# Loading the prompt in eight pieces between the first wide tile's weights, and the gates' tile third

## The chip, the cores and the metric

One core of one Trainium2 chip runs the kernel. The metric is device microseconds of one execution of the whole program. A core has a matmul engine (TensorE, PE in the profile; its weight loads are PEld), VectorE (DVE), ScalarE (ACT), GpSimd (POOL) and SyncE (SP). SP and POOL issue nearly all DMAs here. Each engine takes its own instructions in the order in which the program wrote them and waits on semaphores for the others.

## What is computed

One inference step of a hybrid decoder layer, for a prompt of 512 tokens and a sample group of 32 tokens (8 sequences of 4), in float32, which share the weights:

```python
h = rmsnorm(x, norm_in)                                   # (544, 2048)
z = jnp.einsum('btd,dc->btc', h, w_in)                    # combined input projection
q_n, kv_n, g_n, z_n, q_f, k_f, v_f, f_f, z_f = jnp.split(z, cuts, axis=-1)
gates = jax.nn.sigmoid(g_n + b_gate)                      # 24 columns
logf = jax.nn.log_sigmoid(f_f + b_forget)                 # 8 columns
...                                                       # sparse attention (8 heads), forgetting attention (8 heads)
mix = jnp.concatenate([o_n * jax.nn.silu(z_n), o_f * jax.nn.silu(z_f)], axis=-1)
y = rmsnorm(x + jnp.einsum('btc,cd->btd', mix, w_out), norm_final)
```

The sample group also reads paged caches through a page table (indirect DMAs and DMAs of whole pages).

## The kernel before

**Numbers.** A float32 matmul is written as three matmuls in a faster format: both operands are split into a high part and a low rest (`h_hi`, `h_lo` for the tokens, `whi`, `wlo` for the weights), and `mm3` adds hi x hi, hi x lo and lo x hi.

**Tiles.** The input projection is a list of tiles of 128 output columns each (`tiles`, built by `add_in`). A tile has the 544 tokens in two halves of 272 (`hf`, `HALF`), the 2048 inputs in 16 k-steps (`kk` within `c`, four each), and so 2 x 16 x 3 = 96 wide matmuls into two PSUM banks (`pz`). Tile 0 is different: it holds the 24 gate columns and 8 forget columns, its weights `w_0` are loaded by POOL, and it is multiplied in plain float32, four k-steps side by side on 32 output rows each. Tiles 1 to 4 are keys and values of the sparse branch, tiles 5 to 8 the queries q0 to q3 of the forgetting branch.

**Weights.** The weights of a wide tile come in four slabs of 256 KB (`raw`, five buffers, number m = 4 t + c), loaded by `w_dma` on SP. `w_split(m, 0)` makes `whi` on ACT, `w_split(m, 1)` makes `wlo` on DVE and issues the load of the slab five further on. Slabs are split `W_AHEAD` = 2 ahead of their use.

**Start.** `start` loads the prompt (`xt`), turns it by TensorE transposes (four of 128x128 for each k-step, into a PSUM bank), and from each bank ACT writes `h_hi` and DVE `h_lo`, scaled with the norm's weights. The per-token factor of the RMS norm is left out of `h`; it is made beside it (`ss`, sums of squares; `rstd_of`, Newton steps; `dg` and two matmuls, which copy it over all rows: `rsb`) and multiplied into a tile's result `zt` as it leaves PSUM. A tile that ends before `rsb` is there is copied raw and multiplied later in `post` (`raw_part`).

**Order.** The program is one pass in Python that writes the instructions. `Clock` keeps an estimate of each engine's time, by formulas. `Streams` holds generators for everything beside the tiles; `pump()` continues those whose flags, tests and estimated ready times have come, by the estimated time of TensorE, and `need(...)` lets that time pass until flags are set. A `yield` with nothing waits for the estimated end of what the generator has just issued. So flags such as "x15" (k-step 15 has been written) or "t0" order what is *written*; on the chip only the order within an engine and the semaphores of real data dependences hold. `clock.parts` tells the estimate which parts of a buffer are tracked apart.

**Before, at the start:** `run_tiles(0, n_in)` takes the tiles in the order 0, 1, 2, ... Tile 0 begins when the first four k-steps are there ("begun"), and its c-th quarter needs k-steps 4c to 4c+3. `index_tiles` (page table arithmetic for the gathers) issues the loads of `w_0` first of all. The sums of squares are issued after tile 0 ("t0"), two on DVE, the others on ACT. Tile t is begun when tile t-2's `post` has set its flag, since `zt` has two buffers. `post_gf` turns tile 0's result into gates and forget values, on which `fox_sample_setup` waits ("gf").

Of the kernel before, what the change touches and what calls it, by code (L numbers as in the profile page):

```python
# [8 lines left out]
F32 = mybir.dt.float32  # L9
# [3 lines left out]
OP = mybir.AluOpType  # L13
# [27 lines left out]
class Clock:  # L41
# [19 lines left out]
    def keys(self, ap):  # L61
        k, part = self.key(ap), self.parts.get(ap.tensor.name)
        if not part:
            return [k]
        pitch, step = part
        lo = ap.offset % pitch
        hi = lo + sum(st * (n - 1) for st, n in list(ap.ap)[1:])
        return [(*k, i) for i in range(lo // step, hi // step + 1)]
# [232 lines left out]
def trunk_step(ctx, tc, x_prompt, x_sample, cache_nsa_kv, cache_fox_kv, cache_fox_logf, state_nsa_win,  # L301
# [127 lines left out]
    by_rows(h_hi), by_rows(h_lo)  # L429
# [83 lines left out]
    def run_tiles(t0, t1):  # L513
        for t in range(t0, t1):
            spec = tiles[t]
            if t == 0:
                S.need("begun")
            if t - 2 >= 0:
                S.need(f"post{t - 2}")
# [7 lines left out]
            for c in range(4):  # L527
                m = t * 4 + c
                if t == 0:
                    S.need(*[f"x{c * 4 + kk}" for kk in range(4)])  # L530
                    for hf, cut in enumerate(cuts):
                        sl = slice(*cut)
                        for b in (h_hi, h_lo):
                            for kk in range(4):
                                mm(ps[hf][kk * 32:kk * 32 + 32], w_0[0][:, m * 4 + kk], b[:, c * 4 + kk, sl].bitcast(F32),
                                   c == 0 and b is h_hi, c == 3 and b is h_lo)
                            S.pump()
                    w_split(m + W_AHEAD, 0)
                    w_split(m + W_AHEAD, 1)
                    if c == 3:  # L540
                        for hf, cut in enumerate(cuts):
                            cp(zt[:, slice(*cut)], ps[hf])
                        flags.add("t0")
                    S.pump()
                    continue
                hi, lo = wsp.pop(m)
                for hf, cut in enumerate(cuts):
                    sl = slice(*cut)
                    for kk in range(4):
# [3 lines left out]
                        if kk == 3 and c == 3:  # L553

                            if t > 1:
                                S.need("rsb")
                            elif t == 1:
                                raw_part.append(sl)
                            late = max(clock.t["dve"], clock.t["pe"]) > max(clock.t["act"], clock.t["pe"]) + 0.2
                            if t == 1:  # L560
# [12 lines left out]
            def post(t=t, spec=spec, zt=zt, raw_part=raw_part):  # L573
                yield [zt]
                if t == 1:
                    yield "rsb"
                for sl in raw_part:
                    nc.vector.tensor_tensor(zt[:, sl], zt[:, sl], rsb[:, sl], op=OP.mult)
                if raw_part:
                    yield [zt]  # L580
                yield from spec["post"](zt)
                flags.add(f"post{t}")
            S.add(post(), front=True)
            S.pump()

# [1300 lines left out]
    def start():  # L1886
        with tile_pool("pre") as pre:
            gn = load(pre.tile([KT, P], F32, name="gn"), dram(norm_in, 0, [[P, KT], [1, P]]))
            xs = load(pre.tile([32, D], F32, name="xs0"), dram(x_sample, 0, [[D, 32], [1, D]]))
            xt = pre.tile([P, 4, 4, 512], F32, name="xt")  # L1890
            clock.parts[xt.tensor.name] = (4 * D, D)
# [13 lines left out]
            jk = lambda n: pre.tile([P, 4, 512], F32, name="jk" + n)  # L1905
# [13 lines left out]
            for k in range(KT):  # L1919
                c = k // 4  # L1920
                if k % 4 == 0:
                    yield [xt[:, c]]
# [3 lines left out]
                for i in range(4):  # L1926
                    nc.tensor.transpose(tp[:, i * P:(i + 1) * P], xt[:, c, i, (k % 4) * P:(k % 4 + 1) * P], ident)
# [32 lines left out]
    def index_tiles():  # L1960
        ptb = big().bitcast(I32)[:, :64]
        pid = fsk.tile([64, 1], I32, name="pid")
        w_0.append(fx.tile([P, 1040], F32, name="ft", bufs=2)[:, :512].rearrange("p (k n) -> p k n", n=32))
        for (col, n, at) in tiles[0]["cols"]:
            nc.gpsimd.dma_start(w_0[0][:, :, at:at + n], dram(w_in[0], col, [[w_in.shape[-1], P], [P * w_in.shape[-1], KT], [1, n]]))
# [12 lines left out]
        yield "x11"  # L1978
# [11 lines left out]
        yield "t0"  # L1990
# [49 lines left out]
    if True:  # L2040
# [45 lines left out]
        run_tiles(0, n_in)  # L2086
# [30 lines left out]
```

## Time and profile before

| | |
|---|---|
| median of three runs | 1316.84 us (1313.9 to 1319.7) |
| the profiled execution | 1315.31 us |
| its span, first to last instruction | 1313.6 us |
| mean granted TensorE clock | 0.992 |
| TensorE busy | 1273.6 us, 97% of the span |
| VectorE, ScalarE, GpSimd busy | 60%, 42%, 21% |
| HBM | 235.68 MB read, 36.49 MB written |

Rows of the profile that stand below: a row of stretches gives the stretch, its length, the busy time of PE, PEld, DVE, ACT and POOL with the number of instructions, the granted TensorE clock, the share of the 16 DMA engines that was busy (it can pass 1 by a little) and the GB/s moved. A row of a timeline gives start and length in us, the engine (a q behind it is the engine's sequencer, which issues DMAs), the line, the operation, output<-inputs, shapes, the count, and in brackets how long the engine was idle before it and what ended that. A row of the chain of waits gives start, length and what held the chain then. All lines are L169, since one helper issues every instruction. A plain float32 matmul shows as two records.

### The profile page before, as it was taken

To read this page: it belongs to the slowest core of one execution; us is meant where nothing else is said; L and a number is where in the kernel's file an instruction comes from. 1 tells how busy PE (TensorE), PEld (TensorE's weight loads), DVE (VectorE), ACT (ScalarE), POOL (GpSimd) and SP (SyncE) were. 2 spreads that over 40 slices of the span, in tenths; PEclk is the share of its full clock that TensorE was granted. 3 is DMA by queue.
4 is the path that set the end of the run, shared out by engine and by line. 5 is a ranking of instruction groups with operands and counts; after the bars stand their busy time and mean duration, and the time that the engine had idled before them with its cause. 6 is when DMAs were issued, how large, how long until landed. Compare 5 with 4: busy or idle time off the path is not lost.

```text
span 1313.6 us, 27307 instructions
## 1 busy us (share of the span) xinstructions
PE 1273.6 (97%) x10149; PEld 1136.0 (86%) x10149; DVE 792.3 (60%) x1982; ACT 545.8 (42%) x1163; POOL 280.2 (21%) x357
## 2 busy tenths in 40 slices
PE   7999999999999999998999999899999999999997
PEld 5899998878989999998899988788888898777786
DVE  5836787775545667656687653666575255345256
ACT  4324333333334577741345551357654323333221
POOL 3312376644310000005661013011211000000000
PEclk8999999999999999999999999899999999999999
DMA  7576699989987455459987489996986693334423
GB/s 195 160 195 187 194 289 278 280 239 285 295 249 172 124 154 161 146 150 327 287 254 207 106 261 257 228 224 188 265 209 181 203 326 109 110 113 135 134 75 137
DMA packets 303665, 265.66 MB, mean 202 GB/s; under 512 B 83058, under 2 KB 250850, under 8 KB 302860
## 3 DMA queue, kind: packets, MB, share of 16 engines
q1 hardware_dynamic: 279372, 187.30, 51.1%
q0 software_dynamic: 24016, 76.10, 18.2%
q8 instruction: 79, 1.29, 0.4%
q14 instruction: 54, 0.44, 0.1%
q10 hardware_dynamic: 144, 0.52, 0.1%
HBM read 235.68 MB, written 36.49 MB: 207 GB/s over the span
## 4 chain that ended last, share of the span: by engine, by line
PE 73%; DMA 11%; issue 5%; DVE 4%; POOL 3%; SPq 2%; ACT 2%; POOLq 0%; DVEq 0%; ACTq 0%
PE pz L169 40%; PE po L169 15%; PE tr L169 5%; PE s L169 4%; PE accv L169 3%; PE acc L169 3%; DMA fpg<-in_cache_fox_kv 2%; DMA raw<-in_w_in 2%; POOL fpg L169 2%; DMA fpg<-in_cache_fox_kv,fi 2%; SPq L169 2%; PE accf L169 1%; PE psb L169 1%; DMA fvz<-out 1%; POOL crow L169 1%
## 5 line engine op out<-in xcount | busy, mean ns | idle before, releaser
L169 PE MATMUL pz<-h_hi,whi 128*128 128x272 f32 x1920 | 567.1, 295 | 7.0 <-ACT zt L169 6.4
L169 PE MATMUL pz<-h_hi,wlo 128*128 128x272 f32 x1920 | 555.3, 289 | 3.4 <-DVE wlo L169 3.4
L169 PE MATMUL pz<-h_lo,whi 128*128 128x272 f32 x1920 | 553.9, 289 | 0.0
L169 PEld LDWEIGHTS pz<-h_hi,whi 128*128 128x128 f32 x1920 | 362.7, 189 | 24.6 <-issue 14.4
L169 PEld LDWEIGHTS pz<-h_hi,wlo 128*128 128x128 f32 x1920 | 362.1, 189 | 4.3 <-DVE wlo L169 4.3
L169 PEld LDWEIGHTS pz<-h_lo,whi 128*128 128x128 f32 x1920 | 363.3, 189 | 0.8
L169 ACT ACTIVATE whi<-raw 128x512 fp32r<-128x512 f32 x275 | 171.4, 625 | 236.3 <-PE pz L169 118.7
L169 DVE TENSOR_TENSOR wlo<-raw,whi 128x512 fp32r<-128x512 f32 x275 | 185.9, 677 | 136.9 <-ACT whi L169 134.5
L169 POOL DMA_INDIRECT fpg<-in_cache_fox_kv,fi x128 | 129.7, 1014 | 294.8 <-DMA out<-nat 208.2
L169 DVE STREAM_TRANSPOSE ft<-fpg 128x1024 f32<-128x1024 f32 x64 | 78.5, 1231 | 42.0 <-DMA fpg<-in_cache_fox_kv,fi 36.7
L169 PE MATMUL po<-whi,h_hi 128*128 128x512 f32 (+1 forms) x256 | 95.6, 374 | 0.0
L169 DVE TENSOR_TENSOR zt<-pz,rsb 128x272 f32<-128x272 f32 x67 | 29.6, 441 | 107.9 <-PE pz L169 105.9
L169 PE MATMUL po<-wlo,h_hi 128*128 128x512 f32 (+1 forms) x256 | 94.0, 367 | 0.0
L169 PE MATMUL po<-whi,h_lo 128*128 128x512 f32 (+1 forms) x256 | 93.9, 367 | 0.0
L169 POOL DMA_INDIRECT crow<-in_cache_nsa_kv,ci x64 | 66.3, 1036 | 114.3 <-DVE ct L169 89.8
L169 ACT ACTIVATE cxh<-ct 128x580 fp32r<-128x580 f32 (+1 forms) x64 | 42.2, 660 | 107.2 <-DVE ct L169 92.8
L169 POOL DMA_DIRECT2D spg<-in_cache_nsa_kv x64 | 35.0, 546 | 183.8 <-DVE skt L169 74.0
L169 PEld LDWEIGHTS po<-whi,h_hi 128*128 128x128 f32 x256 | 48.1, 188 | 20.1 <-ACT whi L169 7.6
L169 POOL DMA_DIRECT2D fpg<-in_cache_fox_kv x64 | 35.0, 552 | 133.3 <-PE accv L169 110.3
L169 ACT ACTIVATE zt<-pz 128x272 f32<-128x272 f32 x54 | 21.4, 397 | 88.4 <-PE pz L169 88.4
L169 DVE TENSOR_TENSOR cxl<-ct,cxh 128x580 fp32r<-128x580 f32 (+1 forms) x64 | 46.1, 720 | 16.0 <-ACT cxh L169 15.0
L169 PEld LDWEIGHTS po<-whi,h_lo 128*128 128x128 f32 x256 | 48.2, 188 | 8.7
(412 smaller groups left out, 1936.5 us busy)
## 6 DMA issues: line engine op xcount, KB each, us to landing
raw<-in_w_in SPq DMA_DIRECT2D x240, 256.0 KB
fpg<-in_cache_fox_kv SPq DMA_DIRECT2D x64, 256.0 KB
fpg<-in_cache_fox_kv POOLq DMA_DIRECT2D x64, 256.0 KB
raw<-in_w_out SPq DMA_DIRECT2D x40, 256.0 KB
spg<-in_cache_nsa_kv POOLq DMA_DIRECT2D x64, 128.0 KB
spg<-in_cache_nsa_kv SPq DMA_DIRECT2D x64, 128.0 KB
out<-in_state_nsa_win SPq DMA_DIRECT2D x32, 254.0 KB
scr_z<-zt SPq DMA_DIRECT2D x28, 272.0 KB
```

The source lines that it names most:

```text
L169: return fn(*a, **k)
```

## The change

- The prompt comes in eight loads of 256 columns (512 KB, runs of 1 KB) in place of two of 256 and three of 512 columns. The slabs 4 to 7, tile 1's weights, are loaded in between, one ahead of every second piece; slab 8 follows the last.
- `run_first` multiplies tile 1 first, k-step by k-step as `h_lo` is estimated to be there; `first_splits` splits slabs 4 to 9. Its result leaves PSUM raw.
- Then come tile 2, tile 0, tile 3 and so on (`turn`). A tile waits for the `post` of the tile two turns before it.
- The loads of `w_0` are written after "x15", and the arithmetic of `index_tiles` after slab 9 has been split.
- The sums of squares no longer wait for tile 0; three of the prompt's four are on ACT, one on DVE, each written after the estimated end of the one before.
- `post` moves out of `run_tiles`, and the sample columns of `h_hi` and `h_lo` get a tracked part of their own.

```diff
+    def made(self, ap):
+        return max(self.wr.get(k, (0.0, 0))[0] for k in self.keys(ap)) + self.HOP
...
-    by_rows(h_hi), by_rows(h_lo)
+    for h in (h_hi, h_lo):
+        clock.parts[by_rows(h).tensor.name] += (SEQ,)
...
-    def run_tiles(t0, t1):
-        for t in range(t0, t1):
+    def run_tiles():
+        turn = [1, 2, 0, *range(3, n_in)]
+        for at, t in list(enumerate(turn))[1:]:
             spec = tiles[t]
-            if t == 0:
-                S.need("begun")
-            if t - 2 >= 0:
-                S.need(f"post{t - 2}")
+            if at > 1:
+                S.need(f"post{turn[at - 2]}")
...
                 if t == 0:
-                    S.need(*[f"x{c * 4 + kk}" for kk in range(4)])
...
-                    w_split(m + W_AHEAD, 0)
-                    w_split(m + W_AHEAD, 1)
...
-                            if t > 1:
-                                S.need("rsb")
-                            elif t == 1:
+                            late = max(clock.t["dve"], clock.t["pe"]) > max(clock.t["act"], clock.t["pe"]) + 0.2
+                            if "rsb" not in flags:
                                 raw_part.append(sl)
...
+    def first_splits(done):
+        for m in range(4, 8 + W_AHEAD):
+            yield lambda: len(done) >= m - 6
+            yield [raws[m]]
+            w_split(m, 0)
+            yield [wsp[m][0]]
+            w_split(m, 1)
+            yield [wsp[m][1]]
+            flags.add(f"w{m}")
+
+    def run_first():
...
+        S.add(first_splits(done), front=True)
+        S.need("begun")
+        for c in range(4):
+            S.need(f"w{4 + c}")
+            hi, lo = wsp.pop(4 + c)
+            for hf, sl in enumerate(cuts):
+                for kk in range(4):
+                    k = c * 4 + kk
+                    S.until(lambda: f"x{k}" in flags and clock.made(h_lo[:, k, sl]) <= clock.t["pe"])
+                    mm3(ps[hf], (hi[:, kk], lo[:, kk]), (h_hi[:, k, sl], h_lo[:, k, sl]), k == 0, k == 15)
+                    if kk == 3 and c == 3:
+                        (nc.vector.tensor_copy if hf else cp)(zt[:, sl], ps[hf])
+                    S.pump()
+            done.append(c)
+
+        S.add(post(1, zt, list(cuts)), front=True)
+        S.need(*[f"w{m}" for m in range(8, 8 + W_AHEAD)])
+        S.pump()
...
-            for c in range(4):
-                w = 512 if c else 256
-                for k in range(0, 512, w):
-                    load(xt[:, c, :, k:k + w], dram(x_prompt, c * 512 + k, [[D, P], [P * D, 4], [1, w]]))
-            for m in range(4, 4 + W_RAW):
-                w_dma(m)
+            for c in range(8):
+                if c % 2 == 0:
+                    w_dma(4 + c // 2)
+                load(xt[:, c], dram(x_prompt, c * 256, [[D, P], [P * D, 4], [1, 256]]))
+            w_dma(8)
...
-                if k == 3:
+                if k == 1:
                     flags.add("begun")
-            yield "t0"
+            yield
             nc.scalar.activation(jk("a")[:32].rearrange("p a b -> p (a b)"), xs, AF.Square, accum_out=ss[:32, 4:5])
             for i in range(4):
-                if i % 2 == 0:
+                yield
+                if i != 3:
...
-        w_0.append(fx.tile([P, 1040], F32, name="ft", bufs=2)[:, :512].rearrange("p (k n) -> p k n", n=32))
-        for (col, n, at) in tiles[0]["cols"]:
-            nc.gpsimd.dma_start(w_0[0][:, :, at:at + n], dram(w_in[0], col, ...))
...
-        yield "x11"
+        yield "x15"
+        w_0.append(fx.tile([P, 1040], F32, name="ft", bufs=2)[:, :512].rearrange("p (k n) -> p k n", n=32))
+        for (col, n, o) in tiles[0]["cols"]:
+            nc.gpsimd.dma_start(w_0[0][:, :, o:o + n], dram(w_in[0], col, ...))
+        yield "w9"
...
-        run_tiles(0, n_in)
+        run_first()
+        run_tiles()
```

More of the change, by code (lines that the diff above doesn't have):

```diff
@@ L64, in keys @@
             return [k]
-        pitch, step = part
+        pitch, step, *edge = part
         lo = ap.offset % pitch
         hi = lo + sum(st * (n - 1) for st, n in list(ap.ap)[1:])
-        return [(*k, i) for i in range(lo // step, hi // step + 1)]
+        rows = [(*k, i) for i in range(lo // step, hi // step + 1)]
+        if not edge:
+            return rows
+        a = lo % step
+        b = a + sum(st * (n - 1) for st, n in list(ap.ap)[1:] if st < step)
+        return (rows if a < edge[0] else []) + ([(*k, -1)] if b >= edge[0] else [])
     def ready(self, ap):
         return max(max(self.wr.get(k, (0.0, 0))[0], self.rd.get(k, (0.0, 0))[0]) for k in self.keys(ap)) + self.HOP
+    def made(self, ap):
+        return max(self.wr.get(k, (0.0, 0))[0] for k in self.keys(ap)) + self.HOP
     def packet(self, aps):
@@ L571, in run_tiles, with post @@
                         S.pump()
[L573 to L583, printed above, removed]
-            S.pump()
+            S.add(post(t, zt, raw_part), front=True)
+            S.pump()
+    def post(t, zt, raw_part):
+        yield [zt]
+        if raw_part:
+            yield "rsb"
+        for sl in raw_part:
+            nc.vector.tensor_tensor(zt[:, sl], zt[:, sl], rsb[:, sl], op=OP.mult)
+        if raw_part:
+            yield [zt]
+        yield from tiles[t]["post"](zt)
+        flags.add(f"post{t}")
+    def first_splits(done):
[8 more added lines that the diff above has]
+    def run_first():
+        zt = stg.tile([P, TOK], F32, name="zt", bufs=2)
+        tile_of[zt.tensor.name] = 1
+        clock.parts[zt.tensor.name] = (TOK, HALF)
+        cuts = (slice(0, HALF), slice(HALF, TOK))
+        ps = [psum.tile([P, HALF], F32, name="pz", tag="pz", bufs=2) for _ in cuts]
+        done = []
+        S.add(first_splits(done), front=True)
[15 more added lines that the diff above has]
+        S.pump()
     def run_outputs():
@@ L1889, in start @@
             xs = load(pre.tile([32, D], F32, name="xs0"), dram(x_sample, 0, [[D, 32], [1, D]]))
-            xt = pre.tile([P, 4, 4, 512], F32, name="xt")
-            clock.parts[xt.tensor.name] = (4 * D, D)
-            for c in range(4):
-                w = 512 if c else 256
-                for k in range(0, 512, w):
-                    load(xt[:, c, :, k:k + w], dram(x_prompt, c * 512 + k, [[D, P], [P * D, 4], [1, w]]))
-            for m in range(4, 4 + W_RAW):
-                w_dma(m)
+            xt = pre.tile([P, 8, 4, 256], F32, name="xt")
+            clock.parts[xt.tensor.name] = (4 * D, 1024)
+            for c in range(8):
[3 more added lines that the diff above has]
+            w_dma(8)
             warm = tr_tile([P, 4, P])
@@ L1904, in start @@
             tmp = pre.tile([P, 15], F32, name="tmpx")
-            jk = lambda n: pre.tile([P, 4, 512], F32, name="jk" + n)
+            jk = lambda n: pre.tile([P, 8, 256], F32, name="jk" + n)
             yield [gn]
@@ L1919, in start @@
             for k in range(KT):
-                c = k // 4
-                if k % 4 == 0:
+                c = k // 2
+                if k % 2 == 0:
                     yield [xt[:, c]]
@@ L1926, in start @@
                 for i in range(4):
-                    nc.tensor.transpose(tp[:, i * P:(i + 1) * P], xt[:, c, i, (k % 4) * P:(k % 4 + 1) * P], ident)
+                    nc.tensor.transpose(tp[:, i * P:(i + 1) * P], xt[:, c, i, (k % 2) * P:(k % 2 + 1) * P], ident)
                 g = gT[:, k:k + 1]
@@ L1989, in index_tiles @@
             nc.vector.tensor_copy(w_0[1][q * 32:q * 32 + 32], ident[q * 32:q * 32 + 32, q * 32:q * 32 + 32])
-        yield "t0"
+        yield
         yield [ptb, pid]
```

5 lines of the change are left out of this document (1 added, 4 removed).

## The prediction

> **What bounds the kernel now.** I read the page first, then the busy time by stretches of 40 us, then the chain of waits of the first 120 us, then TensorE's own timeline.
>
> ```profile
> span 1313.6 us, 27307 instructions
> PE 1273.6 (97%) x10149; PEld 1136.0 (86%) x10149; DVE 792.3 (60%) x1982; ACT 545.8 (42%) x1163; POOL 280.2 (21%) x357
> PE 73%; DMA 11%; issue 5%; DVE 4%; POOL 3%; SPq 2%; ACT 2%; POOLq 0%; DVEq 0%; ACTq 0%
> ```
>
> TensorE is busy 97% of the span, so only its idle time and its slow time can be won: 1313.6 - 1273.6 = 40.0 us idle.
>
> ```profile
> 0.00:40.00 40.00, 32.28 (x290) 25.06 (x291) 26.02 (x69) 21.40 (x32) 13.23 (x36) 0.87 0.60 166
> 160.00:200.00 40.00, 40.00 (x367) 36.83 (x367) 30.25 (x47) 12.77 (x29) 27.70 (x28) 1.00 0.96 291
> 240.00:280.00 40.00, 35.98 (x328) 31.50 (x327) 31.24 (x46) 12.32 (x27) 23.96 (x26) 1.00 0.93 276
> ```
>
> Columns: stretch, its length, busy time of PE, PEld, DVE, ACT, POOL, granted clock, DMA share, GB/s. The first stretch has 7.7 us of the idle time and is the one of these with a clock below 1. Of the rest, 4.0 us lie in the last row, where the DMA share is 0.93; the change does not touch that place directly.
>
> ```profile
> 2.27 10.45 DMA xt<-in_x_prompt
> 12.76 1.97 PE pre L169 x8
> 20.43 1.02 PE pre L169 x8
> 67.61 42.95 PE pz L169 x342
> ```
>
> The chain (start, length, what) begins with 10.45 us of the prompt's load. The same eight transposes take 1.97 us right after it and 1.02 us later. The last row prices a wide matmul: 42.95 / 342 = 0.126 us.
>
> ```profile
> 6.21 1.09 PE L169 MATMUL pre<-ident,xt 128*128 128x128 f32 x8
> 12.76 1.97 PE L169 MATMUL pre<-ident,xt 128*128 128x128 f32 x8 [5.46 <-DMA xt<-in_x_prompt]
> 27.81 0.64 PE L169 MATMUL pz<-h_hi,ft 128*32 128x272 f32 x8
> 28.27 0.64 PE L169 MATMUL pz<-h_lo,ft 128*32 128x272 f32 x8
> 32.09 1.15 PE L169 MATMUL tr<-id,zt 128*128 128x32 f32 x10
> 39.30 0.39 PE L169 MATMUL pz<-h_hi,wlo 128*128 128x272 f32 x1 [0.71 <-DVE wlo L169]
> 43.46 1.46 PE L169 MATMUL pre<-dg,ones 128*128 128x512 f32 x4 [1.13 <-DVE dg L169]
> 54.90 0.81 PE L169 MATMUL tr<-lf_p,ones 128*128 128x24 f32 x6
> 60.12 0.29 PE L169 MATMUL pz<-h_hi,wlo 128*128 128x272 f32 x1
> ```
>
> ```profile
> 5.00:6.00 1.00, 1.00 (x18) 1.00 (x17) 0.00 (x0) 0.18 (x1) 1.00 (x4) 1.00 1.04 312
> 7.00:8.00 1.00, 0.30 (x3) 0.06 (x1) 0.30 (x2) 0.96 (x2) 1.00 (x3) 1.00 1.04 221
> 8.00:9.00 1.00, 0.00 (x0) 0.00 (x0) 1.00 (x3) 0.82 (x2) 0.99 (x3) 0.56 1.46 148
> 9.00:10.00 1.00, 0.00 (x0) 0.00 (x0) 0.71 (x2) 0.00 (x0) 0.83 (x3) 0.50 0.71 125
> 13.00:14.00 1.00, 1.00 (x6) 1.00 (x6) 0.00 (x0) 0.09 (x1) 0.71 (x2) 0.50 1.08 398
> 17.00:18.00 1.00, 1.00 (x7) 1.00 (x6) 0.00 (x0) 0.30 (x1) 0.00 (x0) 0.50 1.07 374
> 18.00:19.00 1.00, 1.00 (x10) 1.00 (x9) 0.57 (x1) 0.85 (x2) 0.00 (x0) 0.82 1.12 341
> ```
>
> TensorE idles from 7.30 to 12.76 us, the clock falls to half at about 8 us and comes back at about 18.4 us. So 12.76 to 18.4 us, 5.6 us of work, runs at half speed and costs 2.8 us. The two later gaps (about 0.9 us before 39.30, 1.3 us before 43.46) wait for VectorE.
>
> **The sum for before.** I count from the first prompt transposes (6.21) to the last matmul of tile 2 (60.12, with 0.13 to its successor: 60.2), 54.0 us. The needed work at full clock: 64 transposes, 8 x 1.02 = 8.2; the gates' tile, 16 groups at the step from 27.81 to 28.27, 16 x 0.46 = 7.4; two wide tiles, 192 x 0.126 = 24.2; the gates' transposes 1.1; the statistics' matmuls 1.4; the forget gates' small matmuls (six of them 0.81) 1.2. Together 43.5, so 10.5 us are lost: 5.5 + 2.8 + 0.9 + 1.3.
>
> **The change, part by part.**
>
> *The loads.* Eight loads of 512 KB replace two of 512 and three of 1024 KB, and four weight slabs (256 KB each) stand between. SP issues 12 DMAs up to the last of them where it issued 5.
>
> ```profile
> L169 SPq DMA_DIRECT2D xt<-in_x_prompt x5: 436/507/3293, 1.8 to 4.1; - x5
> ```
>
> An issue takes 0.44 to 0.51 us (shortest and median; the longest, 3.29, is the last, behind a full queue), and a transfer of 1.7 us covers one load's issue and a slab's. Ahead of the first load stands one slab, 0.26 MB / 312 GB/s = 0.8 us, so the first load lands at 7.0 instead of 6.2. Before, 0.79 MB (the sample rows and the first load) were 2.5 us at this rate from 2.3, so 1.4 us lie between the transfer and 6.21. All of it is 0.26 + 1.05 + 4.19 = 5.5 MB, 17.6 us from 2.3, and with 1.5 us behind it the last load lands at 21.4. Bounds: 398 GB/s (row 13:14, where 2 KB runs moved; the new runs are all 1 KB) gives 17.6; 221 GB/s (row 7:8) gives 28.7. I take 22.5, because of the next part.
>
> *The gates' weights.* They are loaded in runs of 96 and 32 bytes by POOL. The change writes these two DMAs behind "x15", but POOL's queue is in order and nothing in it waits for x15.
>
> ```profile
> 1.53 2.49 POOL L169 DMA_DIRECT2D ft<-in_w_in  x2 [0.31 <-issue]
> 4.01 0.56 POOL L169 DMA_DIRECT2D fpg<-in_page_table  x1
> 5.14 1.53 POOL L169 IOTA fpg<- 128x128 f32 x7
> 6.75 0.56 POOL L169 DMA_DIRECT2D bias<-in_b_gate  x1
> ```
>
> The biases' load shows it: it is written behind the gates' tile (still running at 28.27 us) and runs at 6.75. So I expect the two DMAs at about 4.4 us, past only the page table's loads and the iotas. Their traffic moves about 3 us later and still meets the prompt; the slump to 148 and 125 GB/s at 8 to 10 us moves with it and costs about 1.1 us of transfer. The page table's loads come 2.5 us earlier, towards the first load: 0.5 us, so 7.5 for its landing.
>
> *Tile 1 as the prompt lands.* A chunk of two k-steps holds 8 transposes and 12 wide matmuls, 1.02 + 1.51 = 2.5 us at full clock against (17.6 - 0.8) / 8 = 2.1 us of transfer. TensorE, not DMA, paces this stage: from 7.5 eight chunks are 20.3 us, against a last landing of 22.5 plus some 4.8 us (eight transposes 1.0, eviction and split 1.4, 18 matmuls 2.3), 27.3. So waiting costs only at the start, where hf 0 needs the second chunk before hf 1 begins: I take 1.2, between 0.5 and 3.
>
> *The clock.* It fell at 8 us although TensorE had been busy until 7.3, so I expect it to fall here too. Once cold, a chunk takes 5 us and arrives in 2.1, so TensorE stays busy. By the rows it then needs up to 5.6 us, 2.8 us of cost; the least is nothing. I take 2.2, nearer the row than zero.
> [...]
>
> *The statistics.* They no longer wait for the gates' tile, but each square is now issued behind the one before (a yield each), and the next two tiles are evicted raw.
>
> ```profile
> 26.58 2.73 DVE L169 SCALAR_TENSOR_TENSOR h_lo<-pre,gT,h_hi 128x512 fp32r<-128x512 f32 x4
> 30.42 2.29 DVE L169 CUSTOM_DVE_ANT_1 jkd<-xt 128x2048 f32<-128x2048 f32 x1
> 33.27 1.92 ACT L169 ACTIVATE jka<-xt 128x2048 f32<-128x2048 f32 x1
> 30.00:40.00 10.00, 9.29 (x82) 8.40 (x71) 9.35 (x29) 8.26 (x11) 1.14 (x1) 1.00 0.21 55
> 39.17 0.15 DVE L169 TENSOR_SCALAR tmpx<-ss 128x5 f32<-128x5 f32 x1
> 42.53 1.00 DVE L169 TENSOR_SCALAR dg<-ident,rsx 128x128 f32<-128x128 f32 x5
> 44.62 0.79 DVE L169 COPY rsb<-pre 128x512 f32<-128x512 f32 x2 [0.49 <-PE pre L169]
> 50.42 0.78 DVE L169 TENSOR_TENSOR zt<-zt,rsb 128x272 f32<-128x272 f32 x2
> 53.38 0.72 DVE L169 STREAM_TRANSPOSE nat<-zt 128x544 f32<-128x544 f32 x1
> ```
>
> Four squares on ACT (2.1 each with the accumulator read) and one on DVE (2.3) make 10.7; the Newton steps 2.8 (39.17 to 42.0), dg 1.0, matmuls 1.5, rsb 0.8. From the last h_lo at about 25 that is 41.8, with DVE's queue (9.35 of 10 us busy from 30 to 40 before) some 43. Tile 2's second matmul half needs its pz bank free, and tile 0 needs "post1", 1.5 us behind rsb. TensorE ends tile 1 at 7.5 + 20.3 + 2.2 + 1.2 = 31.2 and tile 2 at 43.3. Stall: 1.8, between 0 and 5.
>
> *Nothing:* the split keys of h_hi, `made` and moved functions issue no instruction. The raw eviction of a second tile adds one pair of multiplies on DVE (0.78), beside TensorE. The gates' result, and so the forget gates' setup, comes some 5 us later; the page loads of that branch wait for tiles q0 to q3 (tiles 5 to 8) anyway.
>
> **Sum.** 7.5 + 42.3 (43.5 less the 1.2 of the forget gates, which now come later) + 2.2 + 1.2 + 1.8 = 55.0. Before, the same work was done at 60.2 - 1.2 = 59.0. Gain 4.0, with the ends 7.2 + 42.3 + 0.5 = 50.0 (gain 9.0) and 8.5 + 42.3 + 2.8 + 3 + 5 = 61.6 (loss 2.6). The profiled execution took 1315.31 us (span 1313.6 and 1.7 around it), so 1311.3 by its own time; it stands 1.5 under the median of 1316.84, which makes 1312.8.
>
> **Rivals.**
>
> *More than counted.* TensorE stays warm, or warms in one stretch, and the statistics are in time: gain 8 to 9, 1308.3. For it: the clock was still 1.00 in 7:8, and 17 us of busy work precede the statistics. Against: 8:9 at 0.56 behind a busy stretch.
>
> *Handed back.* In 160 to 280 us the DMA share is 0.93 to 0.96, and TensorE already idles 4 us in its last 40. If those loads start no sooner, TensorE runs 4 us earlier into the same waits: 1316.8. Against it: they follow tiles 5 to 8, which move with TensorE.
>
> *The statistics decide (slower).* The chain of five serial squares holds post1, and tile 0 stands behind it: the point is a stall of 5.8 us (4.0 gained + 1.8 counted), that is post1 beyond 49. For it: before, the last h_lo to rsb took 16 us (29.3 to 45.4) with two squares at a time. With 9 us of stall it would be 1320.0.
>
> *The order has no effect in time:* the gates' weights still collide with the prompt, the last load lands at 28 and tile 1 ends at 33: gain about 1, 1315.8; this lies inside the forecast's lower half.
>
> **How the numbers follow.** Half a per cent is 6.6 us, about what a measurement of this kernel tells from no change. Forecast (gain 1 to 6.6, and its tail) 0.49, more than counted 0.27, handed back 0.14, statistics 0.10. Faster by over 0.5%: 0.27 and 0.03 of the forecast's tail, 0.30. Slower by over 0.5%: 0.06 of the last and 0.02 for waits that a new order brings elsewhere, 0.08. The rest, 0.62, is within. Range: from the larger gain with 3 us of later waits lost or won, 1304.5, to the statistics' case, 1320; the forecast's own is 1309 to 1316.
>
> **What would show it.** Right: the chain's first DMA piece shrinks from 10.45 to about 5, wide matmuls start at about 10 us, tile 1 ends near 31 and the gates' tile near 54; POOL's ft rows stand near 4.4 us; the clock is at half somewhere between 8 and 15. Wrong: a PE row waiting several us for dg or a pz bank near 43, prompt waits over 2 us behind the first chunk, or new idle time in 160 to 330 us that eats the gain.

## The result and the profile after

The changed kernel took 1329.04 us (median of nine runs, 1323.06 to 1331.4) against 1316.84 for the kernel before: ratio 1.0095, interval [1.0078, 1.0112]. That is 12.2 us slower; the forecast was 1312.8, in a range that ended at 1320. The profiled execution took 1329.14 us. All lines of the changed kernel are L177.

The page of the changed kernel, its span and TensorE's busy time:

```profile
span 1326.9 us, 27319 instructions
PE 1283.3 (97%) x10149; PEld 1145.5 (86%) x10149; DVE 789.3 (59%) x1980; ACT 545.4 (41%) x1167; POOL 284.0 (21%) x357
```

The same number of TensorE instructions is busy 9.7 us longer, and the idle time grew from 40.0 to 43.6 us. The same work took longer, because part of it ran at half clock, as the clock column shows. Stretches of the changed kernel:

```profile
60.00:100.00 40.00, 34.35 (x261) 33.54 (x260) 20.04 (x63) 8.76 (x16) 12.65 (x12) 0.91 0.64 172
160.00:200.00 40.00, 38.19 (x323) 35.84 (x322) 31.04 (x48) 11.55 (x25) 25.33 (x25) 0.96 0.83 245
320.00:340.00 20.00, 14.76 (x90) 9.94 (x89) 7.71 (x13) 4.66 (x11) 10.02 (x12) 0.83 0.88 281
```

and of the kernel before:

```profile
60.00:100.00 40.00, 38.86 (x315) 38.60 (x314) 17.44 (x38) 8.47 (x14) 8.40 (x9) 1.00 0.78 199
320.00:360.00 40.00, 38.82 (x293) 32.20 (x292) 19.43 (x33) 13.30 (x28) 15.29 (x20) 1.00 0.93 299
```

Three places lose, each with idle time and a clock below 1 behind it. To see how much each loses I add up TensorE's matmuls in both traces, each at the median step that its shape has in the kernel before, and compare the times at which both have done the same sum. This lag (plus: behind the kernel before) is for the changed kernel, from one execution of each:

```
time in before, us      65    75    85   125   190   313   340   690   1064   1303
lag of after, us      -3.0  +3.8  +5.4  +5.4  +9.7  +7.2 +13.0  +9.7  +13.4  +13.4
```

So the changed kernel is 3.0 us ahead at 65 us, loses 8.4 between 65 and 85 us, 4.3 up to 190 and 5.8 between 313 and 340 us; the other moves, a further loss of 3.7 up to 1064 us among them, give back 2.1 together. Not all of the 3.0 is a gain: the transposes of pages, for which TensorE waits about 1.1 us in either kernel, stand behind this point in the changed kernel and ahead of it in the kernel before (61.55 us). At 60 us, just ahead of them, the lag is -1.7, so the start gained about 1.7 us (the forecast said 4.0).

**The start.** TensorE's rows of the changed kernel:

```profile
9.55 1.97 PE L177 MATMUL pre<-ident,xt 128*128 128x128 f32 x8 [2.38 <-DMA xt<-in_x_prompt]
13.42 1.97 PE L177 MATMUL pre<-ident,xt 128*128 128x128 f32 x8 [1.90 <-DMA xt<-in_x_prompt]
17.14 1.94 PE L177 MATMUL pre<-ident,xt 128*128 128x128 f32 x8 [1.07 <-DMA xt<-in_x_prompt]
23.46 1.03 PE L177 MATMUL pre<-ident,xt 128*128 128x128 f32 x8
48.39 1.43 PE L177 MATMUL pre<-dg,ones 128*128 128x512 f32 x4
74.54 0.64 PE L177 MATMUL tr<-lf_p,tri_le 128*128 128x32 f32 x2 [4.55 <-DVE lf_s L177]
```

The first piece is there at 9.5 us, the next two are waited for, and three groups of transposes run at half speed (1.97 and 1.94 against 1.03). Tile 1 ends at 36.3, tile 2 at 48.4 us. The matmuls of `dg` at 48.39 show no wait, so there is no stall for the statistics; but `dg` itself was finished no sooner (VectorE's row):

```profile
47.38 1.01 DVE L177 TENSOR_SCALAR dg<-ident,rsx 128x128 f32<-128x128 f32 x5
```

The gates' weights are issued where they were expected, and meet the second and third piece (POOL's row, then 1 us stretches):

```profile
4.37 2.36 POOL L177 DMA_DIRECT2D ft<-in_w_in  x2
8.00:9.00 1.00, 0.00 (x0) 0.00 (x0) 0.33 (x1) 0.99 (x2) 0.99 (x3) 1.00 1.09 381
11.00:12.00 1.00, 0.52 (x3) 0.12 (x1) 0.51 (x1) 0.90 (x2) 0.88 (x5) 1.00 1.76 76
12.00:13.00 1.00, 0.00 (x0) 0.00 (x0) 0.96 (x3) 0.24 (x1) 0.82 (x2) 1.00 0.44 92
```

The clock of 1.00 in these rows is not to be taken at its word: this trace has no record of the clock before 21.18 us, where it goes to full, and the column shows 1.00 until then. TensorE's steps show half speed: a wide matmul takes 0.23 us at 19.10 and 0.126 us from 21.7 on, and the transposes 1.97 against 1.03.

**The first loss.** The last of TensorE's rows above waits 4.55 us for `lf_s`, the forget gates. VectorE's and SP's rows of the changed kernel:

```profile
52.76 5.75 SPq L177 DMA_DIRECT2D out<-nat  x8
65.63 5.19 SPq L177 DMA_DIRECT2D cz<-out  x8
72.83 1.25 DVE L177 STREAM_TRANSPOSE more<-cz 128x1024 f32<-128x1024 f32 x1 [6.04 <-DMA cz<-out]
74.29 0.19 DVE L177 TENSOR_TENSOR lf_p<-fpg 128x32 f32<-128x32 f32 x1
74.40 0.15 DVE L177 TENSOR_TENSOR lf_s<-fpg 32x8 f32<-32x8 f32 x1
```

and VectorE's of the kernel before:

```profile
53.19 0.19 DVE L169 TENSOR_TENSOR lf_p<-fpg 128x32 f32<-128x32 f32 x1
82.74 1.25 DVE L169 STREAM_TRANSPOSE more<-cz 128x1024 f32<-128x1024 f32 x1 [3.38 <-DMA cz<-out]
```

The posts of tiles 1 and 2 now end together. Their results go out to memory (eight stores from 52.76) and are read back by the first compression of the sparse branch (`cz`, eight loads from 65.63). VectorE's transpose of `cz` now stands ahead of the forget gates (in the kernel before it runs some 30 us behind them), so VectorE sits 6.04 us behind that round trip, with the forget gates behind it. They run at 74.29 instead of 53.19, and TensorE, which comes to them in its own order at 69.99, waits. Then the clock falls:

```profile
72.00:76.00 4.00, 1.46 (x7) 1.46 (x8) 2.89 (x7) 0.00 (x0) 0.69 (x1) 0.55 0.82 202
76.00:80.00 4.00, 4.00 (x21) 3.66 (x22) 1.43 (x5) 0.63 (x1) 3.09 (x4) 0.60 0.70 205
```

4.55 us of waiting cost some 2.3 us more at half clock (TensorE works at half speed from 74.54 to about 79.2): 6.9 us, the step from -3.0 to +3.8 in the lag. The other 1.6 are the wait for pages that was put off. At 320 to 340 us a wait for whole pages does the same (chain, then waits of 300 to 380 us; in the kernel before the same waits come to 1.5 us there):

```profile
320.01 12.71 DMA fpg<-in_cache_fox_kv
PE accv L177 <- DMA fpg<-in_cache_fox_kv: 5.2, 1, 5.2
```

### The profile page after: what moved, and what is told of

Same layout as the page of the kernel before. It is cut to its first block, busy times and chain, and to the rows that moved or that the text cites. A ratio compares the mean times of both kernels' runs of the same rounds, so it can differ in the third digit from the quotient of the medians.

```text
span 1326.9 us, 27319 instructions
## 1 busy us (share of the span) xinstructions
PE 1283.3 (97%) x10149; PEld 1145.5 (86%) x10149; DVE 789.3 (59%) x1980; ACT 545.4 (41%) x1167; POOL 284.0 (21%) x357
## 4 chain that ended last, share of the span: by engine, by line
PE 73%; DMA 10%; issue 7%; POOL 4%; DVE 3%; SPq 2%; ACT 1%; POOLq 0%; DVEq 0%; ACTq 0%
PE pz L177 39%; PE po L177 15%; PE tr L177 5%; PE accv L177 4%; PE s L177 4%; PE acc L177 3%; POOL fpg L177 3%; DMA raw<-in_w_in 2%; SPq L177 2%; DMA fpg<-in_cache_fox_kv,fi 2%; POOL crow L177 1%; PE psb L177 1%; PE accf L177 1%; DMA xt<-in_x_prompt 1%; DMA fpg<-in_cache_fox_kv 1%
## 5 line engine op out<-in xcount | busy, mean ns | idle before, releaser
L177 PE MATMUL pz<-h_hi,whi 128*128 128x272 f32 x1920 | 570.1, 297 | 7.5 <-ACT zt L177 6.9
L177 PE MATMUL pz<-h_hi,wlo 128*128 128x272 f32 x1920 | 557.0, 290 | 2.5 <-DVE wlo L177 2.2
L177 PE MATMUL pz<-h_lo,whi 128*128 128x272 f32 x1920 | 555.6, 289 | 0.0
L177 PEld LDWEIGHTS pz<-h_hi,whi 128*128 128x128 f32 x1920 | 364.5, 190 | 27.0 <-issue 14.0
L177 PEld LDWEIGHTS pz<-h_hi,wlo 128*128 128x128 f32 x1920 | 363.9, 190 | 3.4 <-DVE wlo L177 3.0
L177 PEld LDWEIGHTS pz<-h_lo,whi 128*128 128x128 f32 x1920 | 365.2, 190 | 0.6
L177 DVE TENSOR_TENSOR wlo<-raw,whi 128x512 fp32r<-128x512 f32 x275 | 186.1, 678 | 132.4 <-ACT whi L177 128.2
L177 ACT ACTIVATE whi<-raw 128x512 fp32r<-128x512 f32 x275 | 171.7, 625 | 225.7 <-PE pz L177 119.4
L177 POOL DMA_INDIRECT fpg<-in_cache_fox_kv,fi x128 | 131.7, 1029 | 314.2 <-DMA out<-nat 215.9
L177 DVE STREAM_TRANSPOSE ft<-fpg 128x1024 f32<-128x1024 f32 x64 | 78.7, 1232 | 35.0 <-DMA fpg<-in_cache_fox_kv,fi 33.9
L177 PE MATMUL po<-whi,h_hi 128*128 128x512 f32 (+1 forms) x256 | 95.6, 373 | 0.0
L177 PE MATMUL po<-wlo,h_hi 128*128 128x512 f32 (+1 forms) x256 | 93.9, 367 | 0.0
L177 PE MATMUL po<-whi,h_lo 128*128 128x512 f32 (+1 forms) x256 | 93.8, 367 | 0.0
L177 DVE TENSOR_TENSOR zt<-pz,rsb 128x272 f32<-128x272 f32 x63 | 27.8, 441 | 106.6 <-PE pz L177 106.5
L177 ACT ACTIVATE cxh<-ct 128x580 fp32r<-128x580 f32 (+1 forms) x64 | 42.2, 660 | 107.7 <-DVE ct L177 93.6
L177 POOL DMA_INDIRECT crow<-in_cache_nsa_kv,ci x64 | 65.0, 1016 | 90.4 <-DVE ct L177 70.1
L177 POOL DMA_DIRECT2D spg<-in_cache_nsa_kv x64 | 35.1, 548 | 185.5 <-DVE skt L177 91.3
L177 ACT ACTIVATE zt<-pz 128x272 f32<-128x272 f32 x58 | 22.9, 395 | 106.1 <-PE pz L177 106.1
L177 POOL DMA_DIRECT2D fpg<-in_cache_fox_kv x64 | 35.2, 551 | 144.2 <-PE accv L177 101.6
L177 PEld LDWEIGHTS po<-whi,h_hi 128*128 128x128 f32 x256 | 48.1, 188 | 20.2 <-ACT whi L177 7.6
L177 DVE TENSOR_TENSOR cxl<-ct,cxh 128x580 fp32r<-128x580 f32 (+1 forms) x64 | 46.1, 720 | 17.7 <-ACT cxh L177 16.8
L177 PEld LDWEIGHTS po<-whi,h_lo 128*128 128x128 f32 x256 | 48.1, 188 | 8.6
```

Of the source, the lines that this page charges most:

```text
L177: return fn(*a, **k)
```

## The experiments

The theory of the first loss is the round trip in VectorE's queue. For the other 8 us there are two: they follow from the late forget branch, or from the order in which everything later is written, which the planner draws anew once the start has changed. Runs for which the same time of the kernel before is given shared a chip, and a ratio is always against the kernel before on that chip.

**e1: the forget gates first.**

```diff
-            yield (f"nkv{kv}0", f"nkv{kv}1")
+            yield (f"nkv{kv}0", f"nkv{kv}1", "gf")
```

In the changed kernel the first compression waits until the forget gates are written.

> The changed kernel, but the compressed branch's read-back (loads of cz and the transposes into more) is written only after the forget gates are done (flag gf). Theory A (VectorE's queue: the transposes into more, which wait 6 us for cz, stand ahead of the forget gates, and TensorE waits for these and cools): the 4.5 us wait at 74 us and the half-speed stretch behind it go, 8 us in all, and what is lost later goes with them in part: 1315 to 1321. Theory B (the gates come too late for the forgetting branch, whose page loads pace TensorE from 160 to 340 us): only the wait itself goes and the later losses stay or grow: 1322 to 1328. Theory C (any rewritten order moves the time by some us either way): no forecast, anywhere from 1312 to 1330.

**e2: the eight loads alone**, in the kernel before: eight pieces with a slab ahead of every second one, tile order and gates as before.

> The kernel before with the eight loads and the slabs in between, and nothing else of the change (tile 0 first, its weights loaded first, squares after it). Theory A: the second k-step pair still waits for a late piece, so about as before, 1314 to 1319, and no wait of TensorE for the forget gates near 55 to 75 us. Theory B: the same, since the gates stay early. Theory C: 1310 to 1325.

**e3 and e4: another estimate.** `HOP`, the estimate's time for handing over between engines, goes from 0.25 to 0.26, in the kernel before (e3) and in the changed one (e4). No instruction is added or taken away; only choices of the planner that hang by a hair fall otherwise.

> The kernel before with one number of the order's estimate changed (a hop between engines at 0.26 us in place of 0.25); the instructions are the same, their order is another in places. Theories A and B: within 3 us of before, 1314 to 1320. Theory C: 5 us or more from it.

> The changed kernel with the same number at 0.26. Theories A and B: 1325 to 1332, with the wait for the forget gates near 74 us still there. Theory C: 1315 to 1335, 5 us or more from the changed kernel.

Measured, with the kernel before at 1314.09 us on that chip:

| run | median, us | ratio and interval |
|---|---|---|
| e1 | 1334.62 | 1.0160 [1.0123, 1.0197] |
| e2 | 1314.68 | 1.0010 [0.9993, 1.0027] |
| e3 | 1338.15 | 1.0203 [1.0167, 1.0240] |
| e4 | 1320.03 | 1.0051 [1.0026, 1.0076] |

```
time in before, us      65    85   125   190   340   690   1064   1303
lag of e1, us         -2.1  -0.8  -0.8  +0.3  -2.9  -1.9  +23.6  +23.6
lag of e2, us         +1.0  +1.0  +1.0  +1.0  -1.3  -1.9   -3.4   -3.4
lag of e3, us         -1.3  -1.3  -1.3  +0.2  -0.7  -0.8  +17.2  +17.2
lag of e4, us         -4.1  +3.3  +3.3  +4.2  +2.7  -2.6   +4.3   +4.3
```

VectorE's rows of e1:

```profile
67.86 0.19 DVE L177 TENSOR_TENSOR lf_p<-fpg 128x32 f32<-128x32 f32 x1
81.79 1.25 DVE L177 STREAM_TRANSPOSE more<-cz 128x1024 f32<-128x1024 f32 x1 [1.53 <-DMA cz<-out]
```

The forget gates run 6.4 us sooner, the wait of 4.55 us and the half clock behind it are gone: of the 8.4 us only the put-off 1.3 are left (lag -2.1 to -0.8). The first loss is shown to be the order on VectorE's queue. The forget gates are still 14.7 us later than in the kernel before (67.86 for 53.19), and no wait of TensorE for them is left: a delay costs nothing until it passes TensorE's own place for them, near 70 us. The losses at 190 and 340 us are gone too, which fits both theories of them. But the time got worse, by some 25 us between 800 and 1060 us, which neither the change nor this edit touches, and came out above every range that was expected. Row 780 to 1070 us of the kernel before, of e1 and of e3:

```profile
780.00:1070.00 290.00, 281.12 (x2472) 244.23 (x2463) 155.24 (x427) 129.73 (x246) 43.60 (x80) 0.99 0.85 229
780.00:1070.00 290.00, 267.52 (x2268) 224.50 (x2267) 144.09 (x404) 121.60 (x239) 43.65 (x80) 0.95 0.81 208
780.00:1070.00 290.00, 270.88 (x2330) 230.45 (x2329) 150.01 (x414) 118.87 (x232) 43.66 (x80) 0.97 0.83 220
```

In e1 no single wait makes this: the longest of TensorE's there are 4.1 us for `zt` and 3.3 us for `kvc`. e3 decides how to read it: it is the kernel before, without any part of the change, and loses 18 us in the same stretch for a hundredth in one estimate. e4 has the first loss (-4.1 to +3.3) but not the losses at 190 and 340 us, although its forget gates are nearly as late (72.91 us, for 74.29 in the changed kernel): behind 85 us it loses 1.0 where the changed kernel loses 8.0. So a late branch is not enough for those. And e2 tells that the loads alone gain nothing at the start: +1.0. The four orders drawn anew (the changed kernel, e1, e3, e4) are all slower than the kernel before, by 6 to 24 us; whether its order is a lucky draw among many, these runs do not show.

**e5 to e18: the later order held.** To measure the change without a newly drawn order, the order in which the kernel before writes its side work was recorded (2,484 steps of 127 generators) and built into the kernels; from tile 6 on, steps are written by that record.

```diff
+SWITCH = 545
+NAMES, REC, LATE = ...
 class Streams:
+    def replay(self):
+        ...
     def pump(self):
+        self.clock.sub += 1
+        if self.clock.main >= SWITCH and (self.ptr < len(REC) or self.pend):
+            return self.replay()
```

The written rows on TensorE of the changed kernel differ from those of the kernel before up to row 6,610 of some 8,230; with the order held, only within the first 390. Four programs were made: the changed kernel with the order held (e5, e10, e14); the same with the edit of e1 (e6, e11, e15, e17); that with the gates' weights behind the last activation load (e7):

```diff
         yield "x15"
         w_0.append(fx.tile([P, 1040], F32, name="ft", bufs=2)...)
+        nc.vector.memset(w_0[0], 0.0)
```

and that with unused transposes, so that TensorE does not idle between the early pieces (e8, e12, e16, e18):

```diff
             for k in range(KT):
                 c = k // 2
+                if k in (0, 2, 4):
+                    warm = tr_tile([P, 4, P])
+                    for q in range(14):
+                        nc.tensor.transpose(warm[:, q % 4, :], ident, ident)
```

> The changed kernel from its start to the sixth tile, and from there on the side work is written in the order that the kernel before has (on TensorE only the first 390 of some 8,230 rows then differ from before; in the changed kernel itself they differ up to row 6,610). Nothing is left out. Theory: the start gains 3, the late forget gates behind VectorE's queue lose 8.3, and all that was lost after 100 us was the other written order: 1314 + 5.3 = about 1319.5, and the lag at equal TensorE work stays near +5 from 100 us to the end. Rival: the later losses (4 us at 160 to 200, 5 us at 320 to 360) come from the branch being late, whatever the order: 1326 to 1329.

> As the run before it, and the first compression waits for the flag of the forget gates, so that its read-back doesn't stand ahead of them in VectorE's queue. Nothing is left out. Theory: the gain of the start stays, the loss of 8.3 us is gone, and the 26 us that the same edit lost between 800 and 1060 us with a free order do not come: 1314 - 2 to - 3 = 1311 to 1312.5, lag near -2.5 all along. Rival: the loss between 800 and 1060 us belongs to the earlier arrival there (data or weights not there yet), not to the order: 1320 or more, with the lag rising in that stretch.

> As the run before it, and the gates' weights are loaded only once the last of the eight activation loads has landed (their buffer is first cleared by VectorE after it). Nothing is left out. If the two weight loads of the gates at 4.4 us slow the activations' loads: the first load lands about 2 us sooner and tile 1 ends 2 to 3 us sooner, 1308.5 to 1311. If what slows them is the page table's load at 1.5 us or the loads themselves: within 1 us of the run before it. If the gates' tile now waits for its weights: slower than that run by up to 2 us.

> As the run before it, with 14 more transposes of the identity on TensorE (their results are not used) ahead of the first, third and fifth chunk of activations, so that TensorE does not idle between the early chunks. If the half clock up to some 20 us is the cold price (chunks of 16 transposes in 1.95 us against 1.03 later): the clock is full from about 13 us and tile 1 ends 2 to 3 us sooner, 1306 to 1309. If the loads set the pace of the early chunks: the waits for the activations grow by what the chunks shrink, and the time stays within 1 us of the run before it.

> The kernel before, with the side work from the sixth tile on written in the recorded order: the same rows in the same order on every engine as the kernel before. Nothing is left out. A control for the record, and a profile of that program on the chip of this comparison: ratio 1.000 within 0.002. If writing from the record did anything by itself, it would show here as a ratio off 1.

> The program of the fifth run again (the changed start, later work in the order of before), with its own control beside it: the chip of the first comparison of this program moved some 50 GB/s less between 100 and 240 us, so that its late branch could hide behind waits for data. Theory: +3 to +6 against before, lag at equal TensorE work rising at the forget gates (65 to 75 us) and then level. Rival, that the later losses come with the late branch whatever the order: +10 or more, with rises at 160 to 200 and 320 to 360 us.

> The program of the sixth run again, beside its own control: the first compression behind the forget gates, later work in the order of before. Theory that the start gains about 3 and only the order lost the rest: 2 to 3 us faster than before, lag at equal TensorE work -2 to -3 from 75 us to the end. Rival, that being ahead is given back where the transfers set the pace (100 to 340 us): lag -2 to -3 at 85 us and 0 by 340, ratio 1.000. Rival, that the loss at 800 to 1060 us belongs to the change: ratio over 1.005.

> The program of the eighth run again, beside its own control: the gates' weights behind the last activation load, idle TensorE filled with unused transposes ahead of three early chunks, the first compression behind the forget gates, later work in the order of before. Theory that the cold clock and the gates' weights take 3 to 4 us of the start: lag -5 to -6 at 60 to 85 us; if the transfers of 100 to 340 us do not take it back, 5 us faster than before, else level with the run before it.

> The changed kernel as it is, beside the runs below on one chip. If the chip is like that of the first comparison (the kernel before at about 1315): ratio 1.009 to 1.010. If its transfers pause between 145 and 240 us (the kernel before at about 1377): a free order that draws differently there, 0.995 to 1.015.

> The program of the fifth and tenth run (changed start, later work in the order of before), here beside the changed kernel itself. Theory: the forget gates behind VectorE's queue cost about 8 and the start gains 3, so +5 against before (ratio 1.004), and 8 us less than the changed kernel itself, whose other 8 are the other order. Rival, that the later losses belong to the late branch: level with the changed kernel itself (1.009).

> The program of the sixth and eleventh run (first compression behind the forget gates as well). Theory: the gain of the start stays, -2 to -3 against before (ratio 0.998), 8 us under the run above. Rival, that the transfers take the lead back by 340 us: level with before (1.000), lag 0 from 340 us on.

> The program of the eighth and twelfth run (gates' weights after the last activation load, unused transposes ahead of three early chunks, compression behind the forget gates, later work as before). Theory: lag -5 to -6 at 85 us; kept to the end -5 (ratio 0.996), the fastest of the four. Rival, that the transfers take it back: level with the run above.

> The program of the sixth, eleventh and fifteenth run. On a chip where the kernel before takes about 1315 and no transfer pauses at 145 to 240 us: if the lead of the start (lag -1 to -2 at 85 us in e1) is kept while the later order is that of before, ratio 0.998 to 0.999; if it is given back to the transfers, 1.000; if the late loss of e1 belongs to the change and not to the order, over 1.005. On a chip of the other kind: 1.000 to 1.001 as before.

> The program of the eighth, twelfth and sixteenth run. On a chip where the kernel before takes about 1315: lag -4 to -6 at 65 to 85 us; kept to the end, ratio 0.995 to 0.997; given back to the transfers of 100 to 340 us, 1.000. On a chip of the other kind: 0.998 to 1.003 as before.

All lines of the four programs are L180.

| program | runs | ratio and interval | before on that chip, us |
|---|---|---|---|
| the kernel before, from the record | e9 | 0.9982 [0.9955, 1.0008] | 1377.58 |
| the changed kernel itself | e13 | 1.0119 [1.0079, 1.0158] | 1378.22 |
| changed, order held | e5 | 1.0038 [1.0012, 1.0065] | 1376.09 |
| | e10 | 1.0051 [1.0023, 1.0079] | 1377.58 |
| | e14 | 1.0014 [0.9984, 1.0044] | 1378.22 |
| and forget gates first | e6 | 1.0009 [0.9983, 1.0034] | 1376.09 |
| | e11 | 1.0008 [0.9981, 1.0035] | 1377.58 |
| | e15 | 1.0001 [0.9974, 1.0028] | 1378.22 |
| | e17 | 1.0002 [0.9976, 1.0027] | 1314.46 |
| and gates' weights late | e7 | 1.0020 [0.9993, 1.0048] | 1376.09 |
| and unused transposes | e8 | 1.0028 [0.9997, 1.0058] | 1376.09 |
| | e12 | 0.9978 [0.9950, 1.0007] | 1377.58 |
| | e16 | 1.0026 [0.9999, 1.0053] | 1378.22 |
| | e18 | 0.9993 [0.9973, 1.0014] | 1314.46 |

On three of the chips the kernel before itself takes some 62 us longer than on the others; what its transfers do there is in the last section. Every ratio is within one chip.

*The order is the larger part.* On one chip the changed kernel itself (e13) stands at 1.0119 and the same start with the order held (e14) at 1.0014; the intervals do not touch, and the late forget gates are in both (75.10 and 76.04 us). On chips of the faster kind the same two edits at the start give 1.0160 with a free order (e1) and 1.0002 with the order held (e17): about 20 us from the written order of later work. In e17 the stretch that cost e1 its time is whole again:

```profile
780.00:1070.00 290.00, 284.73 (x2504) 248.03 (x2504) 156.46 (x429) 131.21 (x250) 43.58 (x80) 0.99 0.88 234
```

*The late forget gates are the smaller part.* With the order held the changed kernel is at 1.0038, 1.0051 and 1.0014, with the forget gates first at 1.0009, 1.0008 and 1.0001: about 4 us apart in the mean. Single pairs of intervals overlap, and on those chips TensorE waits only about 1 us for the forget gates (0.9 in e13, 1.2 in e14), since it is later itself. The 6.9 us of the faster chips rest on e1; with the order held and the forget gates late, no run was made on a chip of the faster kind.

*The gain of the start does not reach the end.* With order and forget gates in place, both programs on the faster kind of chip are level with the kernel before. The lags, with 4.6 us taken out of e18's sum of work for its 42 unused transposes (0.109 us each):

```
time in before, us      75    85   125   190   340   690   1064   1303
lag of e17, us        -2.1  -0.7  +1.0  +1.4  +3.4  +4.6   +0.2   +0.2
lag of e18, us        -3.0  -1.6  -1.6  -1.6  -3.0  -1.4   -0.3   -0.3
```

Behind the put-off wait for pages e17 is 0.7 us ahead, and that is gone by 125 us; one wait of TensorE between 60 and 120 us, for split weights, is most of the 1.7 us lost there:

```profile
PE pz L180 <- DVE wlo L180: 1.4, 1, 1.4
```

e17 falls 4.6 us behind by 690 us and wins 4.4 of them back by 1064. e18 ends level too: it still has a lead of 2.5 us at 650 us and has lost it by 1050. So a lead and a lag of some us both came to nothing between 600 and 1060 us; what takes them back is not shown by one profile of each. The expectations that a lead of 2 us or more is kept to the end all failed, and no version beat the kernel before.

*What the start is bound by.* Moving the gates' weights (e7) does what it should. Stretches of 2 us, e6 and then e7:

```profile
10.00:12.00 2.00, 1.29 (x7) 0.89 (x5) 0.74 (x1) 1.36 (x2) 1.75 (x8) 1.00 1.36 155
12.00:14.00 2.00, 0.74 (x4) 0.74 (x5) 1.36 (x3) 0.01 (x1) 1.53 (x3) 1.00 0.82 200
10.00:12.00 2.00, 2.00 (x12) 2.00 (x11) 0.48 (x1) 1.11 (x2) 0.00 (x0) 0.50 1.11 331
12.00:14.00 2.00, 1.44 (x10) 1.21 (x9) 1.97 (x4) 1.83 (x4) 0.00 (x0) 0.91 1.11 336
```

331 and 336 GB/s instead of 155 and 200: the two loads of the gates' weights (256 KB in runs of 96 and 32 bytes) do slow the activations, together with the small loads and stores behind them in POOL's queue, which e7 puts off with them. The last transposes begin at 23.98 us instead of 29.23. Yet the time does not move. TensorE's and VectorE's rows of e7:

```profile
9.57 3.31 PE L180 MATMUL pre<-ident,xt 128*128 128x128 f32 x16 [3.04 <-DMA xt<-in_x_prompt]
13.94 1.04 PE L180 MATMUL pre<-ident,xt 128*128 128x128 f32 x8
43.09 0.60 PE L180 MATMUL pz<-h_hi,wlo 128*128 128x272 f32 x1 [2.33 <-DVE wlo L180]
48.33 1.10 PE L180 MATMUL pre<-dg,ones 128*128 128x512 f32 x2 [0.70 <-DVE dg L180]
40.01 0.20 DVE L180 TENSOR_SCALAR pid<-pid 64x1 int32<-64x1 int32 x2
40.13 2.29 DVE L180 CUSTOM_DVE_ANT_1 jkd<-xt 128x2048 f32<-128x2048 f32 x1
47.32 1.00 DVE L180 TENSOR_SCALAR dg<-ident,rsx 128x128 f32<-128x128 f32 x5
```

VectorE goes through the page table's arithmetic (its last row is the one at 40.01), then its sum of squares, the Newton steps and `dg`; the split of tile 2's weights stands in the same queue. TensorE, five us ahead, waits for `wlo`, works at half clock from 43.10 to 46.51 us, waits for `dg`, and starts the statistics' matmuls at 48.33: where e6, with the slower start, has them, at 48.53. Up to some 50 us VectorE's queue bounds this order, and a faster arrival of the prompt is worth next to nothing. The unused transposes keep TensorE busy between the early pieces, but cost 4.6 us of its time themselves; it comes to the statistics' matmuls at 49.91 in e8 and at 48.49 in e18, and waits for `dg` in both.

## Why the prediction was wrong

**The step that failed** is the last sentence of *Nothing*: the gates' result "comes some 5 us later; the page loads of that branch wait for tiles q0 to q3 (tiles 5 to 8) anyway". The forget gates ran 21.1 us later (74.29 against 53.19). I looked for who waits for their result, found the page loads, and costed the delay at nothing. I did not ask what stands ahead of them on VectorE once the posts of tiles 1 and 2 end together, and forgot that TensorE itself has their small matmuls in its order: the quoted row of 54.90 was one of them. It cost 6.9 us, 4.55 of waiting and 2.3 at half clock. A delay of 5 us would indeed have been free, and so were the 14.7 us of e1; the 21.1 were not.

**The second** is the size given to a new order: "3 us of later waits lost or won" in the range and 0.02 in the chances. The runs show about 8 us for this change (13.4 less 5.4 in the lag; some 13 us between the medians of e13 and e14 on a slower chip), 20 for the same start with one flag more, and 24 for a hundredth in an estimate. This term alone is wider than the forecast's whole range. Neither step alone accounts for the distance: 1329.0 less 6.9 or less 8 is still above 1320.

**By the terms of the sum.** The first piece was usable at 9.5 us (7.5 said). The waits for pieces were 1.90 + 1.07 = 3.0 (1.2). What is left up to the end of tile 1, 36.3 - 9.5 - 20.3 - 3.0 = 3.5, is the cold clock's term (2.2); the clock was full only from 21.18 us. By the trace 8.7 us of work ran at half speed, which cost 4.3, so the needed work was less than the 20.3 counted. The statistics' stall was 0 (1.8), but by luck: `dg` was ready only at 48.39, and `rsb` after it, where I had `rsb` near 43. On VectorE the page table's arithmetic, which the change puts behind slab 9, stands ahead of the sum of squares. TensorE came to the matmuls of `dg` 5 us late too (48.39 for 43.3), so nothing showed. In e7 tile 1 ended 5 us sooner (31.2 for 36.3), and the rival that the statistics decide came true on a small scale. And I ended the count of the kernel before at 60.2, with 183 of the 192 wide matmuls done; the last nine ran to 63.3, behind transposes of pages at 61.55. The lower end of the range, by its own terms (1316.84 less 9.0 and 3), is 1304.8 and not 1304.5. With all of it the measured terms give 9.5 + 42.3 + 3.5 + 3.0 = 58.3 for 55.0, and by the traces the stage gained about 1.7 us for 4.0.

**What was right:** the gates' weights at 4.4 us and their collision with the prompt, and a start at half clock. That the clock *falls* there was not so in the profiled execution: it had not yet risen (the transposes of the identity ahead of the first piece took 0.214 us each, against 0.109 at full clock in e18). In e17 it had risen (16 small matmuls at 5.28 us took 1.28 us, against 1.89 in the changed kernel) and fell (the first piece's transposes at 9.37 took 1.97 us, against 1.03 at 24.45). The rival "handed back" is what e17 and e18 measure, once order and forget gates are taken out of the way: 1.0002 and 0.9993. Its mechanism was only partly the one given: the lead was smaller than counted, e17's goes to VectorE's splits by 125 us, and e18 still has its lead at 340 us, behind the stretch that the rival names.

## What to carry to other kernels

When a step is moved, list for every engine what is now written ahead of each of its consumers, and look there for round trips through memory: here VectorE's queue stood still for 6.04 us at such a read-back, the forget gates behind it came 21.1 us later than before, and TensorE paid 4.55 us of waiting and 2.3 at half clock. Where a planner writes the order from estimates, first measure how far the time moves when an estimate changes by a hair; compare a change of a few us only with the later order held, or it measures the draw. Before making data come sooner, look for the engine whose queue ends last in that stage: here it was VectorE, and 5 us of earlier data bought nothing.

## What the runs showed of the hardware

The clock fell after short idle times, too. In e7 TensorE idles 2.33 us before 43.09, and the 1 us stretches there read

```profile
42.00:43.00 1.00, 0.00 (x0) 0.00 (x0) 1.00 (x4) 0.00 (x0) 1.00 (x1) 1.00 0.00 0
43.00:44.00 1.00, 0.92 (x4) 0.92 (x5) 0.94 (x4) 0.00 (x0) 0.69 (x2) 0.55 0.04 12
45.00:46.00 1.00, 1.00 (x7) 1.00 (x6) 0.83 (x6) 0.24 (x1) 0.00 (x0) 0.50 1.13 339
46.00:47.00 1.00, 1.00 (x8) 1.00 (x8) 0.62 (x3) 0.68 (x2) 0.00 (x0) 0.74 0.92 266
```

so behind an idle time of 2.33 us TensorE worked 3.4 us at half clock, from 43.10 to 46.51. The clock of 0.74 in 8 to 10 us of e7, and its two rows further up, put an earlier half clock at about 9.0 to 12.4 us; it began 2.4 us into the idle time of 3.04 us before 9.57.

Other idle times went otherwise. In the kernel before the clock fell at 8.12 us, 0.8 us behind TensorE's last work, and was full again at 18.36, after 5.6 us of work without a wait; over the idle time of 1.14 us before 61.55 it stayed full. In the changed kernel the start stayed at half speed up to 21.18 us, with waits of 2.38, 1.90 and 1.07 us in between and 4.0 us of work without a wait at its end. Later it fell at 72.38 us, 2.4 us into the wait for the forget gates, and was full again at 79.20, after 4.7 us of work. How long TensorE has to idle for the clock to fall, and what brings it back, is not shown.

Chips differ. The kernel before, and the same instructions in the same order on one of the slower chips (e9), 140 to 240 us:

```profile
140.00:240.00 100.00, 98.87 (x869) 92.99 (x868) 78.76 (x133) 32.20 (x67) 63.26 (x63) 1.00 0.88 266
140.00:240.00 100.00, 85.33 (x642) 75.65 (x641) 61.53 (x108) 25.57 (x53) 47.62 (x48) 0.92 0.70 208
```

208 against 266 GB/s for the same work. In e9, for example, 0 GB/s moved from 219.8 to 224.2 us. Why was not found.
